# A Hymba layer on one core: splits of weights and blocks taken off GpSimd in the first steps, transposed blocks evacuated by ScalarE and two blocks ahead, rows squared earlier

## The chip, the cores and the metric

The kernel runs on one core of a Trainium2 chip. The metric is the device time of one execution in microseconds; the time given for a kernel is the median of its runs. A profiled execution has, beside its time, a span: from the first to the last instruction of the program that the profiler saw.

## The reference

One decoder layer on a batch of one: 2048 positions, model width 1024, all in float32. The rows of x are RMS-normalised, one input projection makes six groups of 1024 columns, two token mixers work on them (a gated causal convolution of width 3, and a gated linear recurrence with a causal convolution of width 4 in front of it), each mixer's output is normalised per head and multiplied by a SiLU gate, and one output projection leads back to the width of the model, where x is added and the rows are normalised again.

```python
xn = rms_norm(h, ln_g)
proj = jnp.einsum('bsd,de->bse', xn, w_in)              # (2048 x 1024) @ (1024 x 6144)
b_gate, c_gate, x_conv, g_conv, x_lru, g_lru = jnp.split(proj, splits, axis=-1)
y_conv = b_gate * causal_depthwise_conv(c_gate * x_conv, conv_w)
y_conv = headwise_rms_norm(y_conv, 8, conv_out_g) * jax.nn.silu(g_conv)
u = causal_depthwise_conv(x_lru, lru_conv_w) + lru_conv_b
r, i = sigmoid(u @ w_a + b_a), sigmoid(u @ w_i + b_i)   # block-diagonal, 16 heads of 64
a = jnp.exp(8.0 * r * log_sigmoid(lam))
h_t = a_t * h_{t-1} + sqrt(1 - a_t**2) * (i_t * u_t)
y_lru = headwise_rms_norm(h_t, 16, lru_out_g) * jax.nn.silu(g_lru)
h = h + jnp.einsum('bse,ed->bsd', jnp.concatenate([y_conv, y_lru], -1), w_out)
return rms_norm(h, final_g)
```

## The kernel before, in words

**Splits.** A float32 matrix is written as a high and a low part in a format that TensorE multiplies at full rate: the high part is a rounded copy (mostly a cast on ScalarE, tiles `s` for weights and `th` for the normalised input), the low part is what the copy lost (a subtraction of two tensors of 128x512, function `low`, on VectorE or GpSimd; the second half of tile `s` for weights, tiles `tl` for the input). One product of a block of weights with a block of input is three matmuls (`mm`): high by high, high by low, low by high.

**Steps.** A step is a pair of column groups for one slice of 128 channels of one half of the sequence. Steps are numbered n = 0, 1, 2, ... in the order l, a, b, l, a, b, ...: l is the recurrence's input and gate, a the convolution's two inputs, b its outer gate and SiLU gate. From step 3 on a step uses the Strassen-Winograd form with seven products of 2x2 blocks in place of eight; sums of weight blocks are made on VectorE (`s_plan`). What step n needs is prepared during step n - 1, in eight slots of about 2.7 us each: in one slot ScalarE casts a block, and in the same or the next slot its low part is made. Before the change the low parts 0, 4 and 6 of steps 4 to 23 run on GpSimd, whereas parts 1, 2, 3 and 5 run on VectorE. Work of the mixers is put into queues by the same slots (`at`, `tick`): convolutions, gates, the scan and so on are issued on the engines some slots after the product that they need. Each engine works through its own instructions in the order in which the program issues them; that order is written out by hand.

**Start-up.** Steps 0 to 2 are done plainly, with eight products, while the input is still being prepared. Four blocks of the transposed input arrive from memory unnormalised, are scaled by the gain and split (`raw_hi`, `raw_lo`); `products` multiplies them by the weights of step 0, then of step 1, and the row factors are multiplied in later. At the same time rows 512 to 1023 of x (tiles `x`, `norm_rows`) are squared, normalised, and transposed by TensorE against the identity (`turn`): `second(j)` turns the two blocks of column j, evacuates both from PSUM (tiles `traw`; one by ScalarE, one by VectorE before the change), casts both on ScalarE and makes their low parts, one on VectorE and one on GpSimd. It is called for j = 0 in the middle of step 1's products and for j = 1, 2, 3 one block ahead of the products of step 0's second half.

Rows 0 to 511 (tiles `xh`, eight halves of 128x512) are squared with a sum along the row, to get the row factors: before the change four halves on ScalarE and four on VectorE, after the whole of step 1's products. `roots` spreads the factors over the partitions (tile `rr`), and `scaled(j)` multiplies the eight blocks of the first half by gain and factor on VectorE, casts them on ScalarE and makes their low parts on GpSimd. After that come, in this order on TensorE: products 22 and 12 of step 1 (`plain(1, ...)`, with `after1` called at each half of a product), then step 2's four products (`plain(2, ...)`, with `after2`), with two pairs of the gate matmuls of step 0's recurrence in between (line 744, at slots 8 and 10 after its input was there; they need the tiles `st`, which are casts of `u` on ScalarE and subtractions on VectorE). In `after1` the weights of step 2 are cast and split one block at a time, between the sums of input blocks that step 3 will use (`do_bits`: `traw`, `q`, `u`, `rr` and `t` as results of subtractions, each followed by its low part `tl`).

`spin`, `klam` and the loads at the start do not change.

Of the kernel before, what the change touches and what calls it, by code (L numbers as in the profile page):

```python
# [17 lines left out]
P = 128  # L18
# [20 lines left out]
def hymba_kernel(ctx: ExitStack, tc: tile.TileContext, x, xt, w_in, par, lamc, w_gate, w_out, final_g, out):  # L39
# [151 lines left out]
    def s_plan(n, r, dst):  # L191
# [26 lines left out]

        g = nc.gpsimd if PLAIN < n < 3 * KT else None
        return [lambda: (add(2), add(1)),  # L220
# [322 lines left out]
    def turn(c, kt, dst, act):  # L543
        pool, tag = ((pss, "s"), (psu, "u"))[act]
        tp = pool.tile([P, C], F32, tag=tag, name="tp")
        for b in range(NB):
            nc.tensor.transpose(tp[:, b * P:(b + 1) * P], x0[c * NB + b][:, kt * P:(kt + 1) * P], ident)
        g = pt[:, LN_G + kt:LN_G + kt + 1]
        if act:
            nc.scalar.activation(out=dst, in_=tp, func=AF.Copy, scale=g)  # L550
        else:
            nc.vector.tensor_scalar(out=dst, in0=tp, scalar1=g, scalar2=None, op0=ALU.mult)

# [503 lines left out]
    with tc.manual_schedule(engines={ENG.PE, ENG.Activation, ENG.DVE, ENG.Pool, ENG.SP}):  # L1057
# [76 lines left out]
        s_hi(0, 3)  # L1134
        s_lo(0, 3, g)
        for kt in range(NB + 1, 2 * NB):
            raw_hi(kt)
            raw_lo(kt)
        for i in (0, 2, 1, 3):
            s_hi(1, i)  # L1140
            s_lo(1, i, g if i > 1 else None)
        klam_late()
# [20 lines left out]
        lru0(21, raw[0][1], RAW)  # L1163

        def second(j):
            for n, tag in ((1, "tl6"), (3, "th6")):
                tr[j][n] = tp_.tile([P, C], F32, tag=f"{tag}{j}", name="traw")
            for i in range(2):
                turn(1, j + i * NB, tr[j][2 * i + 1], i)
            B12 = T[3, j] = t_tile(3, j)  # L1170
            nc.scalar.copy(B12[0], tr[j][1])
            Tp[j].hi(5)
            low(tr[j][1], B12)
            Tp[j].lo(5, g)

        for part in range(2):
            for j in range(NB):
                if part == 1 and j == 2:
                    second(0)
                products(1, raw[1], part, j, (0, 4))  # L1180

        rs0, rest = [small.tile([P, NB], F32, tag="ss4", bufs=2, name="ss0") for _ in range(2)]
        for b in range(NB):
            for n in range(2):
                v, acc = xh[b][n], (rs0, rest)[n][:, b:b + 1]
                if n:
                    nc.vector.scalar_tensor_tensor(out=v, in0=v, scalar=1.0, in1=v, op0=ALU.mult, op1=ALU.mult,
                                                   accum_out=acc)
                else:
                    nc.scalar.activation(out=v, in_=v, func=AF.Square, accum_out=acc)  # L1190
        tt(rs0, rs0, rest, ALU.add)
# [12 lines left out]
        def scaled(j):  # L1204
            for i in (0, 4):
# [3 lines left out]
                Tp[j].hi(i)  # L1209
                Tp[j].lo(i, g)  # L1210

# [4 lines left out]
        for j in range(NB):  # L1216
            if j + 1 < NB:
                second(j + 1)
            if j == 2:
                roots()  # L1220
                lru0(11, None, rsb[0])
                lru0(21, None, rsb[0])
            if j >= 2:
                scaled(2 * j - 4)
                scaled(2 * j - 3)
            for cc, n in ((c12, 0), (c22, 2)):
                mm(cc, Sp[0], T, n, j, j == 0, False, k=3)
                mm(cc, Sp[0], T, n + 1, j, False, j == NB - 1, k=5)
        lru0(22, c22, None)
        lru0(12, c12, None)  # L1230
# [43 lines left out]
        def after1(s):  # L1274
            s_hi(2, (2, 3, 0, 1)[s])
            do_bits(2)
            s_lo(2, (2, 3, 0, 1)[s])
            if s == 2:
# [9 lines left out]

        def after2(s):
            do_bits(2)  # L1290
            if s in (1, 2, 3, 4, 6, 7):
# [180 lines left out]
```

## Time and profile before

| what | value |
|---|---|
| median of 3 runs | 1314.8 us |
| lowest and highest run | 1314.07 and 1316.62 us |
| profiled execution, its own time | 1316.63 us |
| span of the profiled execution | 1314.6 us |
| TensorE busy | 1286.9 us, 98% of the span |
| VectorE busy | 1045.1 us, 79% |
| ScalarE busy | 747.6 us, 57% |
| GpSimd busy | 219.0 us, 17% |

Times in the profile's rows are in microseconds from the start of the span. A row of the timeline gives the start, the time from the first start to the last end of the instructions in it, the engine (PE is TensorE, DVE VectorE, ACT ScalarE, POOL GpSimd, SP the queue that issues DMAs), the line, the operation, the tiles (out<-in, buffer numbers left out) and their shapes, the count, and in brackets how long the engine was idle before it and what ended that. Instructions overlap a little at their ends, so the pitch from start to start is shorter than the duration shown. The profiled execution took 2.0 us more than its span.

### The profile page before, as it was taken

The numbers are of one execution on the slowest core, as the hardware profiler recorded it, in microseconds if no ns is written. First come the engines' busy times: TensorE is split into PE (matmuls) and PEld (weight loads), VectorE is DVE, ScalarE is ACT, GpSimd is POOL, SyncE is SP. The second block draws the span as 40 slices with busy tenths as digits, with TensorE's granted clock in tenths as the row PEclk, the third lists the DMA queues.
The fourth block names the chain that finished last, engine by engine and source line by source line (L and its number), as shares of the span: only waits on it lengthen the run. The fifth ranks groups of instructions, "written<-read, shape, count | busy, mean of one in ns | idle before, by whom it ended". The sixth has DMA issues, their size and how long they took to land.

```text
span 1314.6 us, 16650 instructions
## 1 busy us (share of the span) xinstructions
PE 1286.9 (98%) x5654; PEld 1058.6 (81%) x5654; DVE 1045.1 (79%) x1314; ACT 747.6 (57%) x1140; POOL 219.0 (17%) x179
## 2 busy tenths in 40 slices
PE   9879999999999999999999999999999999999997
PEld 7657888888888888887888888888888888888886
DVE  7898898989999998977566676667549777659886
ACT  6557767665666758565554545364457433445443
POOL 2502233233333230001010110101011000000000
PEclk9979999999999999999999999999999999999999
DMA  9117888898989889652789999999779897698754
GB/s 351 39 54 273 306 289 279 287 318 299 341 287 346 297 286 334 195 173 61 265 308 292 338 354 325 342 351 368 243 266 321 262 274 254 211 403 302 243 178 160
DMA packets 159685, 357.38 MB, mean 272 GB/s; under 512 B 17136, under 2 KB 51952, under 8 KB 159600
## 3 DMA queue, kind: packets, MB, share of 16 engines
q1 hardware_dynamic: 154992, 340.26, 75.0%
q0 software_dynamic: 4320, 15.73, 3.1%
q8 instruction: 45, 0.74, 0.2%
q14 instruction: 40, 0.33, 0.1%
q10 hardware_dynamic: 288, 0.32, 0.1%
HBM read 219.21 MB, written 137.04 MB: 271 GB/s over the span
## 4 chain that ended last, share of the span: by engine, by line
PE 86%; DVE 3%; ACT 2%; DMA 2%; issue 1%; SPq 0%; DVEq 0%; ACTq 0%
PE bank L1018 84%; PE gate L744 2%; DMA tl<-td 1%; DVE s L162 1%; DMA yd<-gl 1%; ACT s L212 0%; ACT th L1297 0%; DVE ob L162 0%; DMA s<-sd 0%; DVE raw L162 0%; DMA yd<-gb 0%; ACT r L751 0%; DVE t L835 0%; DVE sums L645 0%; DVE r L778 0%
## 5 line engine op out<-in xcount | busy, mean ns | idle before, releaser
L1018 PE MATMUL bank<-th,s 128*128 128x512 f32 x3560 | 1108.0, 390 | 9.7 <-DVE s L162 3.4
L1018 PEld LDWEIGHTS bank<-th,s 128*128 128x128 f32 x3560 | 670.0, 188 | 154.1 <-DVE s L162 4.2
L1018 PE MATMUL bank<-tl,s 128*128 128x512 f32 x1780 | 694.3, 390 | 0.4 <-DVE tl L162 0.2
L1018 PEld LDWEIGHTS bank<-tl,s 128*128 128x128 f32 x1780 | 335.2, 188 | 70.4 <-POOL tl L162 0.6
L162 POOL TENSOR_TENSOR s<-raw,s 128x512 fp32r<-128x512 f32 x62 | 114.5, 1858 | 292.0 <-ACT s L212 231.4
L212 ACT CAST s<-raw 128x512 fp32r<-128x512 f32 x140 | 84.8, 618 | 35.0 <-PE bank L1018 19.4
L162 DVE TENSOR_TENSOR s<-raw,s 128x512 fp32r<-128x512 f32 (+1 forms) x124 | 84.7, 706 | 6.6 <-ACT s L212 5.7
L162 DVE TENSOR_TENSOR s<-s,s 128x512 fp32r<-128x512 f32 x105 | 74.7, 712 | 0.9 <-ACT s L212 0.9
L162 POOL TENSOR_TENSOR gb<-gb,sg 128x1024 f32<-128x1024 f32 x8 | 21.8, 2723 | 299.1 <-ACT sg L675 260.7
L212 ACT CAST s<-s 128x512 fp32r<-128x512 f32 x105 | 65.0, 619 | 7.8 <-DVE s L162 7.8
L162 DVE TENSOR_TENSOR tl<-traw,th 128x512 fp32r<-128x512 f32 x80 | 54.1, 712 | 18.2 <-ACT th L450 14.2
L716 DVE SCALAR_TENSOR_TENSOR u<-xl,pt,u 128x1024 f32<-128x1024 f32 x48 | 63.4, 1321 | 6.5 <-ACT u L712 5.9
L1399 ACT COPY q<-bank 128x512 f32<-128x512 f32 x58 | 33.8, 583 | 48.6 <-PE bank L1018 44.1
L835 DVE SCALAR_TENSOR_TENSOR t<-p,pt,t 128x1024 f32<-128x1024 f32 x32 | 46.5, 1452 | 13.4 <-ACT t L832 12.6
L751 ACT ACTIVATE r<-gate,pt 64x512 f32<-64x512 f32 x64 | 43.8, 685 | 17.4 <-PE gate L744 16.6
L162 DVE TENSOR_TENSOR st<-u,st 64x512 fp32r<-64x512 f32 x64 | 51.2, 799 | 2.0
L162 DVE TENSOR_TENSOR raw<-raw,zr 128x512 f32<-128x512 f32 x64 | 41.1, 684 | 9.6 <-DMA zr<-rsd 9.6
L1403 ACT COPY rr<-bank 128x512 f32<-128x512 f32 x31 | 18.1, 585 | 51.7 <-PE bank L1018 51.6
L162 DVE TENSOR_TENSOR traw<-traw 128x512 f32<-128x512 f32 x60 | 44.2, 741 | 1.4 <-DMA traw<-in_w_out_dram 0.4
L1409 ACT COPY u<-bank 128x512 f32<-128x512 f32 x31 | 18.1, 585 | 47.2 <-PE bank L1018 47.2
L751 ACT ACTIVATE i<-gate,pt 64x512 f32<-64x512 f32 x64 | 43.8, 685 | 1.1
L1403 ACT COPY u<-bank 128x512 f32<-128x512 f32 x27 | 15.8, 585 | 50.0 <-PE bank L1018 48.7
(208 smaller groups left out, 1354.8 us busy)
## 6 DMA issues: line engine op xcount, KB each, us to landing
sd<-s SPq DMA_DIRECT2D x151, 512.0 KB
s<-sd SPq DMA_DIRECT2D x151, 512.0 KB
raw<-in_w_in_dram SPq DMA_DIRECT2D x104, 256.0 KB
raw<-yd SPq DMA_DIRECT2D x64, 256.0 KB
traw<-in_w_out_dram SPq DMA_DIRECT2D x64, 256.0 KB
so<-so SPq DMA_DIRECT2D x22, 512.0 KB
s<-so SPq DMA_DIRECT2D x22, 512.0 KB
yd<-gb SPq DMA_DIRECT2D x32, 256.0 KB
```

Source lines behind the costliest of these rows:

```text
L162: (eng or nc.vector).tensor_tensor(out=out, in0=a, in1=b, op=op)
L212: nc.scalar.copy(dst[i][0], val(i))
L716: nc.vector.scalar_tensor_tensor(out=v["u"], in0=o1[:, 1 + j:1 + j + N2], scalar=lw[j], in1=v["u"], op0=ALU.mult, op1=ALU.add)
L744: nc.tensor.matmul(ps[j], v["gw"][n][:, j, :], v["st"][j][:, sl], start=(n == 0), stop=(n == 1))
L751: nc.scalar.activation(out=g_[hi, sl], in_=v["ps"][j][src], func=AF.Sigmoid, bias=pt[src, bias + k:bias + k + 1])
L835: nc.vector.scalar_tensor_tensor(out=tcur["t"], in0=p[:, 2 + j:2 + j + N2], scalar=cw[j], in1=tcur["t"], op0=ALU.mult, op1=ALU.add)
L1018: nc.tensor.matmul(bank, a[:, js], b, start=start and n == 0, stop=stop and n == 2, skip_group_check=more)
L1399: nc.scalar.copy(q1, bk["A"])
L1403: nc.scalar.copy(u2, bk["A"])
L1409: nc.scalar.copy(rr, bk["A"])
```

## The change

- `s_plan`: the low parts 0, 4 and 6 of the weights of steps 4 to 9 are made on VectorE, in the place in the program where GpSimd's instruction stood. From step 10 on they stay on GpSimd.
- `turn`: both blocks of a column are evacuated by ScalarE.
- Start-up: the low parts of the weights of steps 0 and 1 that GpSimd made, those of `second` and those of `scaled` are made on VectorE. GpSimd makes no low part before step 10's weights.
- Rows 0 to 511 are squared earlier: those of blocks 0 and 1 on ScalarE and block 2 on VectorE after step 0's products, block 3 on ScalarE after step 1's.
- `second(j)` is called two blocks ahead: for j = 0 and 1 in step 1's products, for j = 2 and 3 in those of step 0's second half; `roots` comes after the first half of block 1.
- `scaled` multiplies and casts all eight blocks, and leaves their low parts to `scaled_lo`, which is called in `after1` and `after2` for one column at a time.
- `after1`: step 2's weights are cast and split two at a time and ahead of `do_bits`, in its first two calls.

```diff
-        g = nc.gpsimd if PLAIN < n < 3 * KT else None
+        g = nc.gpsimd if PLAIN + 6 < n < 3 * KT else None
...
-        g = pt[:, LN_G + kt:LN_G + kt + 1]
-        if act:
-            nc.scalar.activation(out=dst, in_=tp, func=AF.Copy, scale=g)
-        else:
-            nc.vector.tensor_scalar(out=dst, in0=tp, scalar1=g, scalar2=None, op0=ALU.mult)
+        nc.scalar.activation(out=dst, in_=tp, func=AF.Copy, scale=pt[:, LN_G + kt:LN_G + kt + 1])
...
-        s_lo(0, 3, g)
+        s_lo(0, 3)
...
-            s_lo(1, i, g if i > 1 else None)
+            s_lo(1, i)
...
+        def squares(b, eng=None):
+            for n in range(2):
+                v, acc = xh[b][n], (rs0, rest)[n][:, b:b + 1]
+                if eng is None:
+                    nc.scalar.activation(out=v, in_=v, func=AF.Square, accum_out=acc)
+                else:
+                    eng.scalar_tensor_tensor(out=v, in0=v, scalar=1.0, in1=v, op0=ALU.mult, op1=ALU.mult,
+                                             accum_out=acc)
+
+        squares(0)
+        squares(1)
+        squares(2, nc.vector)
...
-            Tp[j].lo(5, g)
+            Tp[j].lo(5)
 
         for part in range(2):
             for j in range(NB):
-                if part == 1 and j == 2:
-                    second(0)
+                if part == 1 and j > 1:
+                    second(j - 2)
                 products(1, raw[1], part, j, (0, 4))
...
+        squares(3)
         tt(rs0, rs0, rest, ALU.add)
...
-                Tp[j].lo(i, g)
+
+        def scaled_lo(j):
+            for i in (0, 4):
+                Tp[j].lo(i)
...
         for j in range(NB):
-            if j + 1 < NB:
-                second(j + 1)
-            if j == 2:
-                roots()
-                lru0(11, None, rsb[0])
-                lru0(21, None, rsb[0])
-            if j >= 2:
-                scaled(2 * j - 4)
-                scaled(2 * j - 3)
+            if j + 2 < NB:
+                second(j + 2)
             for cc, n in ((c12, 0), (c22, 2)):
                 mm(cc, Sp[0], T, n, j, j == 0, False, k=3)
                 mm(cc, Sp[0], T, n + 1, j, False, j == NB - 1, k=5)
+                if j == 1 and n == 0:
+                    roots()
+                    lru0(11, None, rsb[0])
+                    lru0(21, None, rsb[0])
+            if j >= 1:
+                scaled(j - 1)
+        scaled(3)
...
         def after1(s):
-            s_hi(2, (2, 3, 0, 1)[s])
+            if s < 2:
+                for i in (2 - 2 * s, 3 - 2 * s):
+                    s_hi(2, i)
+                for i in (2 - 2 * s, 3 - 2 * s):
+                    s_lo(2, i)
+            if s % 2 == 0:
+                scaled_lo(s // 2)
             do_bits(2)
-            s_lo(2, (2, 3, 0, 1)[s])
...
         def after2(s):
+            if s in (0, 2):
+                scaled_lo(2 + s // 2)
             do_bits(2)
```

ScalarE, from the copy of the first turned block on (`traw` <- `tp` is an evacuation, `th` a cast of it, `xh` the squares of a half row). Before:

```order
L550 ACTIVATE traw_476<-tp_483,pt_156 128x512
L1171 CAST th_489<-traw_475 128x512
L260 CAST th_492<-traw_476 128x512
L1190 ACTIVATE xh_259,ss0_509<-xh_259 128x512
L1190 ACTIVATE xh_261,ss0_509<-xh_261 128x512
L1190 ACTIVATE xh_263,ss0_509<-xh_263 128x512
L1190 ACTIVATE xh_265,ss0_509<-xh_265 128x512
L1192 ACTIVATE ss0_509<-ss0_509,eps_163 128x4
```

The same place after the change:

```order
L1167 ACTIVATE xh_259,ss0_439<-xh_259 128x512
L1167 ACTIVATE xh_260,ss0_440<-xh_260 128x512
L1167 ACTIVATE xh_261,ss0_439<-xh_261 128x512
L1167 ACTIVATE xh_262,ss0_440<-xh_262 128x512
L548 ACTIVATE traw_483<-tp_485,pt_156 128x512
L548 ACTIVATE traw_484<-tp_491,pt_156 128x512
L1182 CAST th_497<-traw_483 128x512
L260 CAST th_500<-traw_484 128x512
L548 ACTIVATE traw_511<-tp_513,pt_156 128x512
L548 ACTIVATE traw_512<-tp_519,pt_156 128x512
L1182 CAST th_525<-traw_511 128x512
L260 CAST th_528<-traw_512 128x512
```

Four squares stand ahead of the first evacuation now, each column has two evacuations and two casts on ScalarE, and a second column follows before the root.

VectorE, from the clearing of a small tile behind the eight products of `scaled` on (`s` <- `raw` is a low part of step 2's weights, `tl` one of an input block, `traw` <- `traw` and `q1` sums for step 3, `u` the recurrence's convolution). Before:

```order
L558 MEMSET rs4_704 128x32
L162 TENSOR_TENSOR traw_235<-traw_475,traw_235 128x512
L162 TENSOR_TENSOR traw_475<-traw_476,traw_475 128x512
L162 TENSOR_TENSOR s_712<-raw_526,s_712 128x512
L716 SCALAR_TENSOR_TENSOR u_710<-xl_434,pt_156,u_710 128x1024 x2
L162 TENSOR_TENSOR traw_476<-traw_476,traw_235 128x512
L162 TENSOR_TENSOR tl_716<-traw_235,th_715 128x512
L162 TENSOR_TENSOR q1_748<-traw_235,traw_476 128x512
L162 TENSOR_TENSOR tl_746<-traw_476,th_745 128x512
L162 TENSOR_TENSOR s_741<-raw_528,s_741 128x512
```

The same place after the change:

```order
L554 MEMSET rs4_696 128x32
L162 TENSOR_TENSOR s_704<-raw_548,s_704 128x512
L162 TENSOR_TENSOR s_706<-raw_550,s_706 128x512
L162 TENSOR_TENSOR tl_640<-traw_235,th_639 128x512
L162 TENSOR_TENSOR tl_644<-traw_235,th_643 128x512
L162 TENSOR_TENSOR traw_235<-traw_483,traw_235 128x512
L162 TENSOR_TENSOR traw_483<-traw_484,traw_483 128x512
L712 SCALAR_TENSOR_TENSOR u_702<-xl_434,pt_156,u_702 128x1024 x2
L162 TENSOR_TENSOR s_738<-raw_547,s_738 128x512
L162 TENSOR_TENSOR s_740<-raw_549,s_740 128x512
```

Two low parts of weights come first, and two low parts of scaled blocks stand ahead of the sums of their column.

VectorE during step 3, where step 4's weights are prepared (`s_1099` is the low part 0 of step 4's weights, `r` the scan of the recurrence). Before:

```order
L162 TENSOR_TENSOR s_1080<-s2_870,s_1080 128x512
L162 TENSOR_TENSOR raw_1053<-raw_1052,raw_1053 128x512
L778 SCALAR_TENSOR_TENSOR r_907<-r_907,u_710 128x1024
L781 COPY hl_179<-r_907 128x1
L162 TENSOR_TENSOR gb_825<-gb_825,sg_1088 128x1024
```

The same place after the change:

```order
L162 TENSOR_TENSOR s_1080<-s2_868,s_1080 128x512
L162 TENSOR_TENSOR s_1099<-raw_1052,s_1099 128x512
L162 TENSOR_TENSOR raw_1053<-raw_1052,raw_1053 128x512
L774 SCALAR_TENSOR_TENSOR r_907<-r_907,u_702 128x1024
L777 COPY hl_179<-r_907 128x1
```

One instruction more stands in VectorE's order here; from step 4 to step 9 there are 18 such instructions.

More of the change, by code (lines that the diff above doesn't have):

```diff
@@ L1163, in hymba_kernel @@
         lru0(21, raw[0][1], RAW)
+        rs0, rest = [small.tile([P, NB], F32, tag="ss4", bufs=2, name="ss0") for _ in range(2)]
+        def squares(b, eng=None):
[9 more added lines that the diff above has]
+        squares(2, nc.vector)
         def second(j):
@@ L1173, in second @@
             low(tr[j][1], B12)
-            Tp[j].lo(5, g)
+            Tp[j].lo(5)
         for part in range(2):
             for j in range(NB):
-                if part == 1 and j == 2:
-                    second(0)
+                if part == 1 and j > 1:
+                    second(j - 2)
                 products(1, raw[1], part, j, (0, 4))
[L1182 to L1190, printed above, removed]
+        squares(3)
         tt(rs0, rs0, rest, ALU.add)
```

## The prediction

> **What bounds the kernel now.** The page comes first: TensorE is busy nearly throughout, and its granted clock is full except in one stretch early on.
>
> ```profile
> PE 1286.9 (98%) x5654; PEld 1058.6 (81%) x5654; DVE 1045.1 (79%) x1314; ACT 747.6 (57%) x1140; POOL 219.0 (17%) x179
> PEclk9979999999999999999999999999999999999999
> ```
>
> So only what TensorE waits for can be won. The waits of TensorE, asked for by stretches of 30 to 60 us up to 130 us, and for the rest, name these:
>
> ```profile
> PE bank L1018 <- ACT s L1098: 1.5, 1, 1.5
> ...
> PE gate L744 <- DVE st L162: 5.7, 1, 5.7
> PE bank L1018 <- DVE s L162: 3.4, 2, 2.5
> PE gate L744 <- DVE raw L162: 2.7, 1, 2.7
> ...
> PE bank L1018 <- ACT q L1399: 1.6, 1, 1.6
> PE bank L1018 <- ACT rr L1403: 1.0, 1, 1.0
> ```
>
> They add up to 15.9 us and lie between 57 and 113 us. From 130 to 400 us none is listed. The timeline says who sets them: VectorE's row ahead of each wait, then the end of the wait.
>
> ```profile
> 58.88 0.50 PE L1018 MATMUL bank<-th,s 128*128 128x512 f32 x1 [1.51 <-ACT s L1098]
> 77.74 2.84 DVE L162 TENSOR_TENSOR st<-u,st 64x512 fp32r<-64x512 f32 x4
> 78.57 0.76 PE L744 MATMUL gate<-st,bh 128*128 128x512 f32 x1 [5.67 <-DVE st L162]
> 86.92 1.41 DVE L162 TENSOR_TENSOR traw<-traw 128x512 f32<-128x512 f32 x2
> 87.64 0.62 ACT L1240 CAST th<-traw 128x512 fp32r<-128x512 f32 x1 [2.69 <-DVE traw L162]
> 88.69 0.68 ACT L751 ACTIVATE r<-gate,pt 64x512 f32<-64x512 f32 x1
> 105.70 0.50 PE L1018 MATMUL bank<-th,s 128*128 128x512 f32 x1 [1.56 <-ACT q L1399]
> 112.46 0.50 PE L1018 MATMUL bank<-th,s 128*128 128x512 f32 x1 [1.01 <-ACT rr L1403]
> ```
>
> VectorE works without a pause up to the sum at 86.92; the cast at 87.64 waits for it; the gate's sigmoids (88.69) stand behind that cast on ScalarE, and ScalarE is then a closed chain up to the copies that let TensorE go on at 105.70 and 112.46. So VectorE's queue up to 86.92 sets the start-up's length. What delays that queue:
>
> ```profile
> 32.17 0.68 DVE L1187 SCALAR_TENSOR_TENSOR xh<-xh 128x512 f32<-128x512 f32 x1
> 32.78 0.68 DVE L1187 SCALAR_TENSOR_TENSOR xh<-xh 128x512 f32<-128x512 f32 x1
> 42.24 0.59 ACT L1202 COPY rr<-rsb 128x512 f32<-128x512 f32 x1
> 42.86 1.39 DVE L162 TENSOR_TENSOR xl<-xl,rr 128x512 f32<-128x512 f32 x1 [0.32 <-ACT rr L1202]
> 44.78 10.58 DVE L1207 SCALAR_TENSOR_TENSOR traw<-traw,pt,rr 128x512 f32<-128x512 f32 x8
> 46.26 13.63 POOL L162 TENSOR_TENSOR tl<-traw,th 128x512 fp32r<-128x512 f32 x8 [2.55 <-ACT th L260]
> 55.40 0.62 ACT L260 CAST th<-traw 128x512 fp32r<-128x512 f32 x1 [1.08 <-DVE rs L558]
> 58.86 1.57 DVE L162 TENSOR_TENSOR s<-raw,s 128x512 fp32r<-128x512 f32 x1
> 60.35 2.59 DVE L716 SCALAR_TENSOR_TENSOR u<-xl,pt,u 128x1024 f32<-128x1024 f32 x2
> 63.47 0.68 DVE L162 TENSOR_TENSOR tl<-traw,th 128x512 fp32r<-128x512 f32 x1
> 64.07 0.69 DVE L162 TENSOR_TENSOR q<-traw 128x512 f32<-128x512 f32 x1
> ```
>
> Alone, an instruction of 128x512 has a pitch of 0.61 (32.17 to 32.78) or 0.60 us (63.47 to 64.07). Beside GpSimd's eight subtractions, eight of them take 10.58 us, 1.32 each.
>
> **The change, part by part.** *Squares, transposes, evacuations.* ScalarE and TensorE at the place:
>
> ```profile
> 28.00 0.69 ACT L550 ACTIVATE traw<-tp,pt 128x512 f32<-128x512 f32 x1 [4.13 <-PE tp L547]
> 28.59 0.61 ACT L1171 CAST th<-traw 128x512 fp32r<-128x512 f32 x1
> 29.62 0.63 ACT L1190 ACTIVATE xh<-xh 128x512 f32<-128x512 f32 x1
> ```
>
> Four squares of 0.6 us fit into the idle 4.13 us ahead of 28.00, if their rows have landed. Then four columns of two evacuations (0.59) and two casts (0.51) are 8.8 us, block 3's squares 1.2, root and the copy `xx` with their waits about 1.4: from about 27.6 us to 39.0. So `rr` is copied at 39.0, where it was at 42.24. TensorE isn't in the way: it issues the same transposes and products, and the last two columns it turns before ScalarE has come to them.
>
> *Low parts off GpSimd, `scaled`.* VectorE begins at 39.6 (0.62 after the copy, as before) and has ten instructions at 0.60: done at 45.6, ScalarE's last cast begins at the same time (55.40 before). From that cast to the first low part of step 2 it took 58.86 - 55.40 = 3.46 us; the same instructions stand in between now, so VectorE goes on at 49.1. That is 9.8 us earlier. It is idle for 3.4 us, which costs nothing that could be seen elsewhere.
>
> *Step 2's weights first, `scaled_lo`.* From there to the `st` rows VectorE has 28 instructions of half width (16.8 us at 0.60), three `u` of full width (2.52 a pair, 3.8 in all) and one product of full width (1.15): 21.75; for dependent pairs 0.8 (the pair at 86.92 takes 1.41), for a wait on ScalarE's casts behind a table load 0.5, for GpSimd's two gate splits 0.5. So `st` begins at 72.6 instead of 77.74, and the first gate's matmul at 73.4. TensorE ran out of step 1's products at 58.88 - 1.51 = 57.4 and has 36 matmuls of step 2 ahead of the gate, at 0.23 each (1286.9 us over 5654) 8.2 us; it reaches the gate at about 64 to 65.6. So the waits for step 2's weights (1.5 and 3.4) go, and the wait at the gate grows from 5.7 to 8 or 10. Behind `st` the instructions up to the row at 86.92 repeat, with two more low parts (1.2): the pair that ScalarE waits for begins at 72.6 + (86.92 - 77.74) + 1.2 = 83.0, against 86.92. Gain 3.9, taken as 4.0 (the pieces are good to 0.1 or 0.2 each). From there on every row repeats 4 us earlier, the waits of 2.7, 1.6 and 1.0 us included; slow matmuls after the long wait are hidden, as the second gate waits for ScalarE anyway.
>
> *Steps 4 to 9.* VectorE gets 18 low parts of 0.60, 10.8 us, and loses GpSimd's company. What that company costs, grouped from 112 to 245 us, and the same kinds alone:
>
> ```profile
> L716 DVE SCALAR_TENSOR_TENSOR u<-xl,pt,u 128x1024 f32<-128x1024 f32 x8 | 11.8, 1474 | 0.1
> L778 DVE TENSOR_TENSOR_SCAN r<-r,u 128x1024 f32<-128x1024 f32 x3 | 8.8, 2941 | 0.1
> L162 DVE TENSOR_TENSOR s<-raw 128x512 f32<-128x512 f32 x7 | 8.7, 1236 | 0.0
> L162 DVE TENSOR_TENSOR s<-s,raw 128x512 f32<-128x512 f32 x6 | 7.1, 1178 | 0.2
> L835 DVE SCALAR_TENSOR_TENSOR t<-p,pt,t 128x1024 f32<-128x1024 f32 x4 | 7.0, 1742 | 0.3
> ...
> 113.76 0.68 DVE L162 TENSOR_TENSOR raw<-raw 128x512 f32<-128x512 f32 x1
> 114.36 2.28 DVE L778 TENSOR_TENSOR_SCAN r<-r,u 128x1024 f32<-128x1024 f32 x1
> 117.88 1.28 DVE L657 SCALAR_TENSOR_TENSOR u<-r,pt,gl 128x1024 f32<-128x1024 f32 x1
> ```
>
> Against 1.28, 2.28, 0.68, 0.68 and 1.28 the five groups are longer by 1.6, 2.0, 3.9, 3.0 and 1.8: 12.3 us. So what is added and what falls cancel, and TensorE, which doesn't wait here, goes on so. I take 0, or a little below: one bubble of 0.3 us near 137, behind a late `u`, should close. A new wait stands in VectorE's order, for ScalarE's cast of the same block; behind it are queued the sums and the reads of PSUM. In the steps where the sigmoids fill ScalarE it holds VectorE for 2 to 3 us, which the idle share there covers:
>
> ```profile
> 150.00:169.00 19.00, 19.00 (x86) 15.73 (x85) 15.87 (x15) 18.13 (x29) 7.13 (x5) 1.00 0.90 334
> ...
> sum 151.50, PE 151.50 PEld 125.00 DVE 139.56 ACT 104.91 POOL 46.82; mean PE 30.30 PEld 25.00 DVE 27.91 ACT 20.98 POOL 9.36
> ```
>
> In the first of these rows, of the fullest stretch, VectorE is busy for 15.87 and ScalarE for 18.13 of 19.00 us; the second sums five windows from 112.5 to 264 us.
>
> The Trainium skill speaks against such a relief: "Advanced Engine Details and Errata", section "VectorE Performance Modes", has GpSimd and VectorE block each other where VectorE runs in a mode with two ports, and "VectorE: DVE Perf Modes", section "Why `tensor_tensor` can't do 2×_2P or 4×", says that a sum of two tensors never does. By that rule the relief would be 0 and the sum that of rival 1. The trace disagrees: the groups of 1236 and 1178 ns are such sums, against 0.68 us alone.
>
> *Low parts of steps 0 and 1.* Three move to VectorE before 18 us; they fall where it waits for ScalarE's casts or where nothing is due, so 0.
>
> *Sum.* -4.0 - 0.3 + 0 = -4.3 us. The profiled execution took 1316.6 us (span 1314.6), so 1312.3 by it; it was the highest of the runs, and I put the difference on their median: 1314.8 - 4.3 = 1310.5.
>
> **The rivals.**
> 1. *The relief fails (slower).* VectorE gets 10.8 us in steps 4 to 9 and four holds of about 2.4 us behind casts, but stays as slow as now. By the five windows it has 151.5 - 139.6 = 11.9 us to spare, so 10.8 + 9.6 - 11.9 = 8.5 us reach TensorE, less 4.3: about 1319. It decides as soon as the relief is below half of 12.3 us. The 10.58 us speak against it; for it, that GpSimd often ran slow itself, and that the holds lie in the fullest steps. The skill's rule above would lead here. Chance 0.10.
> 2. *The rows land late (no change).* The four squares head ScalarE's queue; if `xh` lands only as late as 29.6, where the first square ran without waiting for it, all evacuations move by 3.3 us, `rr` is no earlier than it was, and about 0.7 to 1.3 us are left: near 1314. Against it: their loads were issued behind the rows squared by 22 us. Chance 0.13.
> 3. *More comes back (faster).* ScalarE's chain behind 88.69 is shortened as VectorE's sums come sooner, and the waits of 1.6 and 1.0 us fall too: 1308. Against it: in the trace that chain is ScalarE's own work. Chance 0.07.
>
> That the change doesn't do what it says is excluded: in the instructions' order GpSimd has no low part before step 10.
>
> **How the numbers follow.** The forecast, 1310.5 with 1309 to 1312 for the uncertain pieces, has the rest, 0.70. The range, 1307.5 to 1314.2, takes in rivals 2 and 3 and leaves rival 1 out. 0.2% is 2.6 us, about what a measurement can tell here: faster means below 1312.2. That is rival 3 and nearly all of the forecast (0.75); within it lie rival 2 and the forecast's weak end (0.16); slower is rival 1 but for its mildest part (0.09).
>
> **What would show it.** Right: `rr` copied near 39, `scaled`'s products in a row of about 5 us, no wait for step 2's weights, one wait of 8 to 10 us at the first gate, ending near 73; the waits of 2.7, 1.6 and 1.0 us still there, 4 us earlier; no wait of TensorE from 110 to 260 us. Wrong: squares that wait for DMA, VectorE's rows above 0.7 us without GpSimd beside them, or new waits in steps 4 to 9.

## The result and the profile after

The changed kernel takes 1311.02 us (median of 7 runs, 1310.72 to 1312.18), the kernel before 1314.8 (median of 7 runs, 1314.01 to 1316.64). The ratio is 0.9969, 95% interval 0.9959 to 0.9979: faster by 0.31%. The profiled execution took 1311.02 us, with a span of 1309.2.

The waits of TensorE in the changed kernel, from 60 to 100, from 100 to 130 and from 130 to 400 us:

```profile
PE gate L740 <- DVE st L162: 9.5, 1, 9.5
PE gate L740 <- ACT i L747: 3.1, 2, 2.9
PE bank L1014 <- DVE tl L162: 1.0, 1, 1.0
...
PE bank L1014 <- ACT rr L1416: 1.0, 1, 1.0
PE bank L1014 <- ACT q L1412: 0.9, 1, 0.9
...
PE bank L1014 <- ACT q L1412: 0.3, 1, 0.3
```

The waits for step 2's weights are gone, the wait at the first gate (the first of the two groups of gate matmuls, line 740 here) has grown from 5.7 to 9.5 us, and the waits behind it are still there. The timeline of the changed kernel:

```profile
26.50 1.03 PE L547 MATMUL tp<-ident,x 128*128 128x128 f32 x8
38.18 0.61 ACT L1205 COPY rr<-rsb 128x512 f32<-128x512 f32 x1
40.24 5.39 DVE L1210 SCALAR_TENSOR_TENSOR traw<-traw,pt,rr 128x512 f32<-128x512 f32 x8
49.12 1.29 DVE L162 TENSOR_TENSOR s<-raw,s 128x512 fp32r<-128x512 f32 x2 [3.46 <-ACT s L1094]
72.85 0.77 PE L740 MATMUL gate<-st,bh 128*128 128x512 f32 x1 [9.50 <-DVE st L162]
82.40 1.41 DVE L162 TENSOR_TENSOR traw<-traw 128x512 f32<-128x512 f32 x2
107.91 0.50 PE L1014 MATMUL bank<-th,s 128*128 128x512 f32 x1 [1.01 <-ACT rr L1416]
```

Against the rows of before: the roots' copy `rr` 42.24 to 38.18, the eight products 10.58 to 5.39 us, the pair of sums that ScalarE waits for (called the pair from here on) 86.92 to 82.40, the last wait of the start-up 112.46 to 107.91. One row of the kernel before belongs beside these, TensorE's first transposes, which stand at the same place in its order in all kernels here:

```profile
26.93 1.04 PE L547 MATMUL tp<-ident,x 128*128 128x128 f32 x8
```

They began 0.43 us earlier in the changed kernel's execution. A shift of that size comes without an edit: in the experiment whose program is that of before up to there (steps 4 to 9 alone) they began at 28.11, and over the twelve experiments anywhere from 26.82 to 28.11. So what is compared from here on is the **start-up's length**, from these transposes to the end of the last wait at the copy of `rr`: 112.46 - 26.93 = 85.53 us before, 107.91 - 26.50 = 81.41 after. That is 4.12 us less. Behind it, up to the end of the span, before has 1314.6 - 112.46 = 1202.1 us, the changed kernel 1309.2 - 107.91 = 1201.3; over the experiments, one execution each, this part lies between 1200.0 and 1203.0, as wide a spread as many of the differences in the table below.

The gain doesn't show as less waiting alone. Over the start-up TensorE's idle time falls from 16.9 to 15.6 us, and its busy time from 68.6 to 65.8, for the same work: most of that is a slow stretch of the kernel before, at 66 us behind a wait for step 2's weights, which the changed kernel doesn't have.

Steps 4 to 9, as busy time from 112 to 245 us before and from 107.5 to 240.5 us after (behind the length, the columns are TensorE, its weight loads, VectorE, ScalarE, GpSimd, each with its count, then clock, DMA share, GB/s):

```profile
112.00:245.00 133.00, 132.54 (x583) 109.31 (x584) 121.61 (x136) 94.22 (x145) 41.25 (x29) 1.00 0.82 291
```

```profile
107.50:240.50 133.00, 132.25 (x582) 109.17 (x583) 115.98 (x152) 92.42 (x141) 7.95 (x10) 1.00 0.80 287
```

VectorE does 16 instructions more in 5.6 us less. The groups of sums and of scans that were 1178 and 2941 ns are these now, and what VectorE waits for most there is ScalarE's casts, five times, at most 3.0 us:

```profile
L774 DVE TENSOR_TENSOR_SCAN r<-r,u 128x1024 f32<-128x1024 f32 x3 | 6.9, 2289 | 0.1
L162 DVE TENSOR_TENSOR s<-s,raw 128x512 f32<-128x512 f32 x6 | 4.2, 692 | 0.2
```

```profile
DVE s L162 <- ACT s L212: 11.6, 5, 3.0
```

### The profile page after: what moved, and what is told of

Read it like the earlier page. It is cut to its first block, busy times and chain, and to the rows that moved or that the text cites. A ratio compares the mean times of both kernels' runs of the same rounds, so it can differ in the third digit from the quotient of the medians.

```text
span 1309.2 us, 16631 instructions
## 1 busy us (share of the span) xinstructions
PE 1283.7 (98%) x5654; PEld 1058.7 (81%) x5654; DVE 1036.1 (79%) x1339; ACT 751.2 (57%) x1148; POOL 164.3 (13%) x146
## 4 chain that ended last, share of the span: by engine, by line
PE 78%; DMA 6%; DVE 5%; ACT 3%; issue 2%; SPq 0%; DVEq 0%; ACTq 0%
PE bank L1014 75%; DMA tl<-td 2%; PE gate L740 2%; DVE s L162 2%; DMA s<-so 1%; DMA zr<-rsd 1%; DVE tl L162 1%; DMA fg<-in_final_g_dram 1%; ACT s L212 1%; DMA traw<-in_w_out_dram 1%; DVE ob L162 0%; DVE raw L162 0%; DVE sums L641 0%; ACT th L1310 0%; DMA yd<-gl 0%
## 5 line engine op out<-in xcount | busy, mean ns | idle before, releaser
L162 DVE TENSOR_TENSOR s<-raw,s 128x512 fp32r<-128x512 f32 (+1 forms) x144 | 96.9, 695 | 19.6 <-ACT s L212 15.6
L162 POOL TENSOR_TENSOR s<-raw,s 128x512 fp32r<-128x512 f32 x42 | 78.8, 1889 | 192.2 <-ACT s L212 133.0
L162 DVE TENSOR_TENSOR tl<-traw,th 128x512 fp32r<-128x512 f32 x92 | 61.7, 709 | 21.0 <-ACT th L450 14.2
L1412 ACT COPY q<-bank 128x512 f32<-128x512 f32 x58 | 33.9, 584 | 48.7 <-PE bank L1014 43.7
```

What stands on the lines that cost most here:

```text
L162: (eng or nc.vector).tensor_tensor(out=out, in0=a, in1=b, op=op)
L1412: nc.scalar.copy(q1, bk["A"])
```

## The experiments

The theory: VectorE's queue up to the pair (82.40 in the changed kernel) sets the start-up's length, one for one, and the part of the change in steps 4 to 9 is worth nothing. The rivals: ScalarE's or TensorE's own work sets the length; or the gain came from steps 4 to 9. Each experiment edits the changed kernel unless it says otherwise. The start-up's length is worked out from two rows of each kernel's timeline, the end of the last wait less the first transposes; they are shown where more than the table hangs on them. The kernel before ran again beside each group of experiments, with medians of 1315.07 us (the first four), 1315.73 (the next three and step 2's weights one at a time) and 1316.19 (the rest); each ratio is to the runs beside it, so ratios can be compared across the table, and medians less well.

| kernel | median us | ratio to before, 95% | start-up | against the change |
|---|---|---|---|---|
| before | 1314.8 | 1 | 85.53 | +4.12 |
| changed | 1311.02 | 0.9969 (0.9959-0.9979) | 81.41 | 0 |
| before, steps 4 to 9 off GpSimd | 1315.4 | 1.0000 (0.9991-1.0009) | 85.48 | +4.07 |
| steps 4 to 9 back on GpSimd | 1310.55 | 0.9965 (0.9952-0.9977) | 81.49 | +0.08 |
| four extra low parts | 1315.52 | 0.9997 (0.9989-1.0006) | 83.82 | +2.41 |
| low parts into VectorE's pause | 1308.59 | 0.9946 (0.9933-0.9959) | 78.60 | -2.81 |
| low parts on GpSimd | 1312.89 | 0.9979 (0.9970-0.9988) | 81.84 | +0.43 |
| an evacuation on VectorE | 1311.33 | 0.9969 (0.9959-0.9979) | 81.54 | +0.13 |
| transposes one block ahead | 1314.49 | 0.9985 (0.9977-0.9994) | 83.43 | +2.02 |
| squares at their old place | 1313.76 | 0.9982 (0.9973-0.9991) | 83.99 | +2.58 |
| step 2's weights one at a time | 1309.08 | 0.9951 (0.9938-0.9963) | 79.66 | -1.75 |
| the same, 20 idle transposes | 1309.26 | 0.9950 (0.9937-0.9962) | 78.97 | -2.44 |
| roots one block earlier | 1306.92 | 0.9932 (0.9920-0.9945) | 78.05 | -3.36 |
| the same, 20 idle transposes | 1307.81 | 0.9940 (0.9927-0.9953) | 76.90 | -4.51 |

A microsecond is 0.0008 of the ratio, and the intervals are some 0.001 to either side; the start-up's length, read in one execution, is good to about 0.1 us, by the two pairs of kernels that differ only behind it (81.41 and 81.49, 85.53 and 85.48); two pairs are all there is for that. The two columns agree within the intervals.

### Steps 4 to 9, undone alone

```diff
-        g = nc.gpsimd if PLAIN + 6 < n < 3 * KT else None
+        g = nc.gpsimd if PLAIN < n < 3 * KT else None
```

> The changed kernel with the low parts of steps 4 to 9 back on GpSimd. The forecast's term for these steps is 0 (18 low parts of 0.60 added, 10.8 us; GpSimd's company gone, 12.3 us): without it VectorE's groups from 108 to 245 us are back at 1.2 us for a sum of 128x512, TensorE waits for at most 0.3 us more, and the time is that of the changed kernel, 1311.0, by 0.5 at most to either side. If the move itself is a loss that something else covers (the relief is smaller than what is added), the time falls by 1 to 4 us, to 1307 to 1310. If the gain of the change came from here, it rises to about 1314.8.

```profile
26.98 1.03 PE L547 MATMUL tp<-ident,x 128*128 128x128 f32 x8
108.47 0.50 PE L1014 MATMUL bank<-th,s 128*128 128x512 f32 x1 [1.03 <-ACT rr L1416]
```

Its ratio is 0.9965 against 0.9969, and the start-up is the same within 0.08 us.

### Steps 4 to 9, done alone on the kernel before

```diff
-        g = nc.gpsimd if PLAIN < n < 3 * KT else None
+        g = nc.gpsimd if PLAIN + 6 < n < 3 * KT else None
```

> The kernel before with one edit: steps 4 to 9 off GpSimd. The start-up is as before, the row that was at 112.46 stays there within 0.2 us. By the forecast's term the time is that of before, 1314.8, or 0.3 less. If the relief fails, VectorE gets 10.8 us and the holds behind casts, and the time is 3 to 8 us longer. If the gain came from here, it is near 1311.

```profile
28.11 1.03 PE L547 MATMUL tp<-ident,x 128*128 128x128 f32 x8
113.59 0.50 PE L1018 MATMUL bank<-th,s 128*128 128x512 f32 x1 [1.03 <-ACT rr L1403]
```

The ratio is 1.0000. So this part is worth 0 from both sides, within 0.1% of the time: the gain isn't there, and the relief doesn't fail either.

### A dose in VectorE's queue

Four low parts are computed a second time between step 2's weights and the sums. By then the rows of the first block have been overwritten, so the low parts that step 2 reads are others than the reference's; the work on each engine is the same.

```diff
                 for i in (2 - 2 * s, 3 - 2 * s):
                     s_lo(2, i)
+            if s == 1:
+                for j in range(NB):
+                    Tp[j].lo(0)
```

> The changed kernel with four low parts computed twice, 128x512 each, put into VectorE's queue behind step 2's weights, ahead of the st rows. If VectorE's queue sets the start-up's length, four times 0.60 come through one for one: st at 74.4, the pair at 84.8, the last wait ends at 110.3, time about 1313.4. If another engine sets it, the queue has slack and less than 0.8 us arrive.

```profile
26.84 1.03 PE L547 MATMUL tp<-ident,x 128*128 128x128 f32 x8
110.66 0.50 PE L1014 MATMUL bank<-th,s 128*128 128x512 f32 x1 [1.02 <-ACT rr L1419]
```

Four times 0.60 is 2.4, and the start-up is longer by 2.41 us: one for one. The time rose by more, from a ratio of 0.9969 to 0.9997, some 3.7 us, give or take 1.8 by the two intervals; the rest lies behind the start-up, where this profiled execution took 1203.0 us against 1201.3. From 116 to 1290 us TensorE waits there for 3.2 us in all, against 1.1 in the changed kernel. Nothing that was added runs there, and what made those waits isn't settled.

### VectorE's pause filled

```diff
         scaled(3)
+        for j in range(NB):
+            scaled_lo(j)
         lru0(22, c22, None)
...
-            if s % 2 == 0:
-                scaled_lo(s // 2)
...
-            if s in (0, 2):
-                scaled_lo(2 + s // 2)
```

> The changed kernel with the eight low parts of the scaled rows moved ahead into VectorE's pause of 3.46 us behind the scaled rows, instead of between the sums later. If VectorE's queue up to the pair at 82.40 sets the start-up's length, six of the eight (3.6 us) leave the part of the queue that counts, two only fill what was a wait at 55.88: st begins at 69.6 or earlier, the pair at 78.8, the last wait of the start-up ends at 104.3, and the time is 3.6 us below the changed kernel's, about 1307.4. If ScalarE's or TensorE's own work sets it, the pair may come earlier, but the row at 107.91 does not, and the time stays within 0.6 us of 1311.0.

```profile
27.22 1.04 PE L547 MATMUL tp<-ident,x 128*128 128x128 f32 x8
79.55 1.41 DVE L162 TENSOR_TENSOR traw<-traw 128x512 f32<-128x512 f32 x2
95.49 0.59 ACT L807 COPY gb<-bank 128x512 f32<-128x512 f32 x1 [0.65 <-PE bank L1014]
105.82 0.50 PE L1014 MATMUL bank<-th,s 128*128 128x512 f32 x1 [1.03 <-ACT rr L1414]
```

From the first transposes the pair is at 52.33 instead of 82.40 - 26.50 = 55.90: 3.57 earlier, as forecast. At the end 2.81 are left. Nearly all of the other 0.76 is lost at the copy of `gb`, one of those in ScalarE's closed chain, which now waits 0.65 us for TensorE; in the changed kernel it doesn't wait. So a second bound lies close behind VectorE's: TensorE's matmuls behind the second gate (below).

### Low parts of the scaled rows on GpSimd again

```diff
                 Tp[j].hi(i)
+                Tp[j].lo(i, nc.gpsimd)
...
-            if s % 2 == 0:
-                scaled_lo(s // 2)
...
-            if s in (0, 2):
-                scaled_lo(2 + s // 2)
```

> The changed kernel with the eight low parts of the scaled rows on GpSimd again, each behind its cast, instead of on VectorE later. If GpSimd's company is what stretched VectorE's products, the eight take about 10.6 us instead of 5.39, VectorE goes on at 54.5 instead of 49.1, and has eight instructions (4.8 us) less up to the pair at 82.40: the pair is 0.6 to 2 us later, the time 1311.6 to 1313. If the company costs VectorE nothing and only the number of its instructions counts, the pair is 4.8 us earlier and the time about 1306.2.

```profile
26.90 1.03 PE L547 MATMUL tp<-ident,x 128*128 128x128 f32 x8
40.65 10.59 DVE L1210 SCALAR_TENSOR_TENSOR traw<-traw,pt,rr 128x512 f32<-128x512 f32 x8
108.74 0.50 PE L1014 MATMUL bank<-th,s 128*128 128x512 f32 x1 [1.03 <-ACT rr L1413]
```

The same eight products take 10.59 us beside GpSimd and 5.39 without it, so the company is what stretches them. But the eight low parts on VectorE cost nearly as much as the company did where the change puts them: the move is worth 0.43 us. In VectorE's pause, as in the experiment before, the same eight are worth 3.24 us against this kernel (81.84 - 78.60).

### One evacuation of two on VectorE

```diff
-        nc.scalar.activation(out=dst, in_=tp, func=AF.Copy, scale=pt[:, LN_G + kt:LN_G + kt + 1])
+        g = pt[:, LN_G + kt:LN_G + kt + 1]
+        if act:
+            nc.scalar.activation(out=dst, in_=tp, func=AF.Copy, scale=g)
+        else:
+            nc.vector.tensor_scalar(out=dst, in0=tp, scalar1=g, scalar2=None, op0=ALU.mult)
```

> The changed kernel with one evacuation of each block's two back on VectorE. By the forecast's step, ScalarE's chain sets rr: it loses four evacuations of 0.59, 2.4 us, but TensorE transposes the roots only at 36.9, so rr is copied at 37.5 instead of 38.18, and 0.7 us come through at most: 1310.3 to 1311. If VectorE is late with the evacuations, behind low parts that wait for ScalarE's casts, rr is up to 2.4 us later, and the time up to 1313.4.

The start-up is 0.13 us longer, about what one execution can tell: who evacuates doesn't matter here. The 2.4 us taken off ScalarE's queue don't bring `rr` forward (38.66 - 26.82 = 11.84 us behind the first transposes, 11.68 in the changed kernel): ScalarE now waits 0.52 and 0.55 us for transposes and 0.27 and 0.89 us for VectorE's evacuations.

### Transposes one block ahead

```diff
-                if part == 1 and j > 1:
-                    second(j - 2)
+                if part == 1 and j == 2:
+                    second(0)
...
-            if j + 2 < NB:
-                second(j + 2)
+            if j + 1 < NB:
+                second(j + 1)
```

> The changed kernel with the transposes one block ahead, as they were. ScalarE is idle for 2.3 us longer ahead of its first evacuation (29.4 instead of 27.13), and the fourth block's two evacuations and two casts, 2.2 us, come behind the copy of rr, among the casts that the scaled rows need. By the forecast's step, the last cast is about 2.2 us later, and so are VectorE's next rows and the end: about 1313.2. If the order of the transposes doesn't matter, because the rows are scaled in VectorE's own pace, the time stays within 0.6 us of 1311.0.

```profile
27.57 1.03 PE L547 MATMUL tp<-ident,x 128*128 128x128 f32 x8
37.71 0.59 ACT L1205 COPY rr<-rsb 128x512 f32<-128x512 f32 x1
41.64 1.26 ACT L548 ACTIVATE traw<-tp,pt 128x512 f32<-128x512 f32 x2
45.43 3.93 ACT L260 CAST th<-traw 128x512 fp32r<-128x512 f32 x6 [1.50 <-DVE traw L1210]
111.00 0.50 PE L1014 MATMUL bank<-th,s 128*128 128x512 f32 x1 [1.03 <-ACT rr L1416]
```

2.02 us longer. Half of the working was wrong: the first evacuation isn't later, since the first block is transposed at the same place in both orders, and `rr` comes even 1.5 us earlier from the transposes (10.14 against 11.68). But the fourth block's evacuations (41.64) stand among the casts that the scaled rows need, and the last of these ends 2.0 us later (49.36 - 27.57 against 46.28 - 26.50).

### Squares at their old place

```diff
-        squares(0)
-        squares(1)
-        squares(2, nc.vector)
...
-        squares(3)
+        for b in range(NB):
+            for n in range(2):
+                v, acc = xh[b][n], (rs0, rest)[n][:, b:b + 1]
+                if n:
+                    nc.vector.scalar_tensor_tensor(out=v, in0=v, scalar=1.0, in1=v, op0=ALU.mult, op1=ALU.mult,
+                                                   accum_out=acc)
+                else:
+                    nc.scalar.activation(out=v, in_=v, func=AF.Square, accum_out=acc)
```

> The changed kernel with the rows squared where they were, after step 1's first products and half on VectorE, half on ScalarE. ScalarE has four squares (2.4 us) behind the second block's casts where it now has two (1.2), and is idle ahead of its first evacuation instead. By the forecast's step, rr is 1.2 us later (39.4 instead of 38.18), and so is the end: 1312.2. If the squares set nothing, because VectorE or TensorE's roots come last there, it stays within 0.4 us of 1311.0. Together with the transposes (2.7 us, by the run with them one block ahead) this should make up the 4 us by which rr came earlier.

```profile
28.05 1.03 PE L547 MATMUL tp<-ident,x 128*128 128x128 f32 x8
36.80 0.30 ACT L1199 ACTIVATE ss<-ss,eps 128x4 f32<-128x4 f32 x1 [1.10 <-DVE ss L162]
41.83 0.61 ACT L1209 COPY rr<-rsb 128x512 f32<-128x512 f32 x1
112.04 0.50 PE L1014 MATMUL bank<-th,s 128*128 128x512 f32 x1 [1.03 <-ACT rr L1420]
```

`rr` is 2.1 us later from the transposes (13.78 against 11.68), not 1.2: beside ScalarE's two squares more, VectorE's four, queued behind the second block's low parts, come last, and ScalarE's root waits 1.10 us for their sums. The pair is later by the same 2.10 us (86.05 - 28.05 = 58.00 against 55.90), the start-up 2.58 us longer; most of the difference is a wait of 0.36 us for TensorE at the copy of `gb`.

### Step 2's weights one at a time

```diff
-            if s < 2:
-                for i in (2 - 2 * s, 3 - 2 * s):
-                    s_hi(2, i)
-                for i in (2 - 2 * s, 3 - 2 * s):
-                    s_lo(2, i)
+            s_hi(2, (2, 3, 0, 1)[s])
             if s % 2 == 0:
                 scaled_lo(s // 2)
             do_bits(2)
+            s_lo(2, (2, 3, 0, 1)[s])
```

> The changed kernel with step 2's weights split one at a time, each low part behind the sums of its place, as before. By the forecast the same instructions stand ahead of the pair at 82.40, so it stays there within 0.3 us; TensorE waits again for these weights, at about 57 and 62 us, and for as much less at the first gate; st is 0.6 us earlier at most; the time stays within 0.6 us of 1311.0. If the weights' order is a gain of its own, TensorE's waits for them, 1.5 to 3.4 us, come on top: 1312.5 to 1314.4.

```profile
27.05 1.04 PE L547 MATMUL tp<-ident,x 128*128 128x128 f32 x8
46.15 1.25 DVE L162 TENSOR_TENSOR tl<-traw,th 128x512 fp32r<-128x512 f32 x2
49.69 0.69 DVE L162 TENSOR_TENSOR s<-raw,s 128x512 fp32r<-128x512 f32 x1 [0.96 <-ACT s L1094]
106.71 0.50 PE L1014 MATMUL bank<-th,s 128*128 128x512 f32 x1 [1.03 <-ACT rr L1413]
```

Neither answer: the start-up is 1.75 us shorter, 0.9951 against 0.9969. With the weights' low parts behind other work, VectorE does two low parts and two sums (46.15 to 48.7) while ScalarE gets to the casts, and waits 0.96 us instead of 3.46. So this part of the change is a loss that the other parts cover. Nor is it this order that took away TensorE's waits for these weights: they don't come back here, and the first gate waits for `st` for 7.0 us, where it was 9.5.

### Roots one block earlier, and idle transposes

The next kernel keeps the weights one at a time, puts the second block's scaled low parts behind the first's, transposes the roots one block earlier and scales the first block ahead of the fourth block's low parts (`product` is the multiplying half of `scaled`). The diff is against the kernel with the weights one at a time.

```diff
+            if j == 1:
+                product(0)
             if j + 2 < NB:
                 second(j + 2)
...
-                if j == 1 and n == 0:
+                if j == 0 and n == 0:
                     roots()
...
-            if s % 2 == 0:
-                scaled_lo(s // 2)
+            if s == 0:
+                scaled_lo(0)
+                scaled_lo(1)
```

> Step 2's weights one at a time again, the second block's scaled low parts right behind the first's, and the roots transposed one block earlier with the first block scaled ahead of the fourth block's low parts. If VectorE's queue is still what counts, rr is copied at 36.5 and the eighth product ends at 43.9 instead of 45.6 (1.7 us), a pause of 0.96 us behind it is filled, and both come on top of the 2 us of the weights' order: the pair at 77.8, time about 1306.5. If ScalarE's casts or TensorE's wait for the roots come last there instead, little of the 2.6 us arrives: 1308 to 1309.

```profile
27.86 1.03 PE L547 MATMUL tp<-ident,x 128*128 128x128 f32 x8
84.86 0.63 PE L1014 MATMUL bank<-th,s 128*128 128x512 f32 x1
85.28 0.63 PE L1014 MATMUL bank<-tl,s 128*128 128x512 f32 x1
95.57 0.59 ACT L807 COPY gb<-bank 128x512 f32<-128x512 f32 x1 [1.03 <-PE bank L1014]
105.91 0.50 PE L1014 MATMUL bank<-th,s 128*128 128x512 f32 x1 [1.03 <-ACT rr L1421]
```

This kernel has the lowest median of all, 1306.92 us, 0.9932 (0.9920 to 0.9945): it beats the kernel before and, with intervals that don't overlap, the changed one. Of the forecast 2.6 us beyond the weights' order 1.61 reach the end of the start-up; ScalarE's copy of `gb` now waits 1.03 us for TensorE.

Then the second bound itself, by 20 transposes that nobody reads, on TensorE ahead of the second gate, on this kernel and on the one before it:

```diff
             v["ps"] = ps = []
+            if i == 1 and not full[0]:
+                full[0] = 1
+                spin(20)
```

> The same, with 20 more transposes of the identity on TensorE ahead of the second gate, where it waits for 2.9 us. They compute nothing that is used. If the wait is what brings the granted clock down behind it, the 14 matmuls from the second gate on have a pitch of 0.23 instead of 0.43 us, TensorE is 2.8 us earlier there, ScalarE's copy of gb doesn't wait for it, and the time is 0.6 us below that of the kernel without them, about 1305.9. If the longer wait at the first gate sets the clock, nothing changes; if the transposes run at the slow clock, 0.16 us each as at the start, they take 3.3 us and the second gate is 0.4 us later.

```profile
27.28 1.04 PE L547 MATMUL tp<-ident,x 128*128 128x128 f32 x8
78.76 2.34 PE L541 MATMUL spin<-ident 128*128 128x128 f32 x20
83.82 0.39 PE L1017 MATMUL bank<-th,s 128*128 128x512 f32 x1
84.04 0.39 PE L1017 MATMUL bank<-tl,s 128*128 128x512 f32 x1
93.86 0.58 ACT L810 COPY gb<-bank 128x512 f32<-128x512 f32 x1
104.18 0.50 PE L1017 MATMUL bank<-th,s 128*128 128x512 f32 x1 [1.03 <-ACT rr L1424]
```

> The kernel with step 2's weights one at a time, 1309.1, and the same 20 transposes ahead of the second gate. As above: 0.6 us less, 1308.5, with a pitch of 0.23 us behind the second gate, if the wait of 2.9 us sets the clock; 1309.1 and a pitch of 0.43 if it doesn't; 1309.5 if the transposes themselves run slow.

```profile
27.88 1.04 PE L547 MATMUL tp<-ident,x 128*128 128x128 f32 x8
106.85 0.50 PE L1017 MATMUL bank<-th,s 128*128 128x512 f32 x1 [1.01 <-ACT rr L1416]
```

Behind the filled wait the pitch is 0.22 us (83.82 to 84.04) where it was 0.42 (84.86 to 85.28), ScalarE no longer waits at `gb`, and the start-up is 1.15 and 0.69 us shorter. The pair didn't move against the kernels without the transposes, and now all that it is ahead of the changed kernel arrives at the end (4.53 us ahead, 4.51 arrive; 2.47 and 2.44). The mechanism is as forecast.

The times don't show it (0.9940 against 0.9932, 0.9950 against 0.9951): a microsecond is as large as the intervals, and behind the start-up these profiled executions took 1201.8 and 1201.2 us against 1200.5 and 1200.6. The traces show one place where the gain goes, near 240 us. TensorE's wait there in the kernel with the roots earlier, first without and then with the transposes:

```profile
PE bank L1014 <- ACT q L1417: 0.4, 1, 0.4
PE bank L1017 <- ACT q L1420: 1.6, 1, 1.6
```

In the kernels with the weights one at a time it is 0.20 and 1.35 us. Some 6 us ahead of it VectorE, whose sum `xl` ScalarE needs before that copy `q`, waits to write over `gl` until the DMA that stores it (`yd` <- `gl`) is done: 3.96 and 3.73 us in the two filled kernels, at most 2.79 in the twelve others. That store is issued as much earlier as the start-up gained, but VectorE goes on only 5.7 and 5.5 us after its issue, where it was 4.5 and 4.3. So a third bound stands behind the second. Why the store takes longer stays open.

## Why the prediction was right, step by step

*The bound.* Right. VectorE's queue up to the pair sets the length: 2.4 us put in come out as 2.41, and what is taken out moves the pair by as much (3.57 of 3.6). The limit of this, which the forecast put down as "hidden", is TensorE's slow stretch behind the second gate; it was hidden in the changed kernel, and takes 0.7 to 1.2 us as soon as VectorE is 2.5 us faster. One sentence ahead of it doesn't hold as an account: "So only what TensorE waits for can be won." Its waits got 1.4 us shorter, and the other 2.8 us of the gain stand in its busy time.

*Squares, transposes, evacuations; `rr` at 39.0.* It came at 38.18, 0.4 of it by the execution's earlier transposes. The squares at the head of ScalarE's queue waited for nothing, so rival 2, late rows, fell. The step put its working on ScalarE's queue as a whole, which is only partly so: 2.4 us of evacuations off that queue brought `rr` no earlier. The runs give the parts, each put back alone: squares 2.58, transposes 2.02, evacuations 0.13 us.

*Low parts off GpSimd.* The products came in 5.39 us, where a row of about 5 was forecast; VectorE on at 49.12, forecast 49.1. As a net move it is worth 0.43 us, since its price, eight low parts in the same queue, is paid 5 to 35 us later.

*Step 2's weights first.* The step that failed: of the pause of 3.4 us, which its step before names, the forecast said that it "costs nothing that could be seen elsewhere". It had the pause in its sum, so the number didn't suffer, but the pause stands in the very queue that sets the length. Filling it gave 2.81 us, and the weights' old order, which nearly closes it, 1.75. The waits for these weights went, but not by their order: they are gone in the old order too.

*Sum of the start-up.* 4.0 forecast, 4.12 measured from the first transposes (4.55 from the span's start). The parts undone one by one add up to 3.5 us (2.58 + 2.02 + 0.43 + 0.13 + 0.08 - 1.75); they overlap and need not add up to the whole, and the low parts of `second` and of steps 0 and 1 were not put back alone.

*Steps 4 to 9.* 0 forecast, 0 measured, from both sides. The relief was larger than put down: by the means of the groups, the five that the forecast counted gave 11.2 us where it had 12.3, and four that it left out (the low parts `s` <- `s,s` and `st` above all) gave 4.7, about 16 us in all. The holds of 2 to 3 us came (11.6 us in five), and TensorE never waited for VectorE there; so rival 1 fell.

The prediction read the Trainium skill too narrowly when it took a relief of 0 from it. "VectorE: DVE Perf Modes", section "Why `tensor_tensor` can't do 2×_2P or 4×", says that such a sum needs the second port for its second tensor, and "Advanced Engine Details and Errata", section "VectorE Performance Modes", that GpSimd shares this port. So the two sections leave room for the slowdown, and the trace shows it: a sum took 1178 ns in the kernel before, and 692 without GpSimd's low parts.

*The bubble of 0.3 us near 137* closed; another of about the same size stands at 240.

*The time.* -4.3 forecast, on a median of 1314.8; the medians differ by 3.8, the ratio says 4.1 (2.8 to 5.4). Rival 3, more than the start-up, isn't seen: ScalarE's chain behind the pair took as long as before (107.91 - 82.40 = 25.51 us against 112.46 - 86.92 = 25.54).

## What to carry to other kernels

Find the one queue that sets a stage's length, and count as cost every pause in it, also one that a later wait of the busiest engine seems to cover: there a low part in a pause is free, and a split that "goes first" only to wait for its cast is not. Moving small work from a helper engine to the one that it slows down can come out at nothing, so price both sides before moving it. And where an execution's start shifts by a microsecond, compare from an instruction that every version shares.

## What the runs showed of the hardware

Beside GpSimd's subtractions VectorE's work on two float32 tensors took up to twice as long, products and sums alike: 10.59 and 5.39 us for the same eight products, 1178 and 692 ns for a sum of 128x512 in steps 4 to 9, and 2941 and 2289 ns for a scan of 128x1024.

TensorE slows behind waits of less than 3 us. In the twelve kernels that wait for 2.3 to 3.5 us at the second gate, 3 to 12 matmuls of 512 columns behind it had a pitch of 0.43 instead of 0.23 us, and none had once 2.34 us of the wait were filled with transposes; the granted clock over the start-up rose with that from 0.93 to 0.98 and from 0.89 to 0.96. The Trainium skill ("TensorE: Matmul & The Clock Gate", section "HAM oscillation — how this bites in real kernels") puts the limit at idle gaps of about 3.4 us; the traces have it happen below that.

The length of one wait doesn't decide it. How many matmuls stay slow differs from kernel to kernel behind the same wait (3, 7, 10 and 12 behind 2.92 us in the kernels with four extra low parts, the changed one, the weights one at a time, the roots earlier). And behind the same two waits for step 2's weights, 1.5 and 0.9 us, the execution of the kernel before went on at full pitch (from 60.48), while the one with steps 4 to 9 alone off GpSimd was at 0.43 us from 62.20 to 65.18. What decides was not tested.
